# The second token half's input of the first norm, loaded with features on partitions

## The chip, the core and the metric

The kernel runs on one core of one Trainium2 chip. A core has five engines that run their own instruction streams: TensorE (PE in the profile, with its weight loads shown apart as PEld), VectorE (DVE), ScalarE (ACT), GpSimd (POOL) and SyncE (SP, which here issues most of the DMA transfers). On-chip memory has 128 partitions. The metric is the device time of one execution in microseconds; the kernel before takes 1170.82 us, the median of three runs.

## The reference, cut to what matters

One layer on 1024 tokens of 1024 features. The mixer has four gated-DeltaNet heads (projections q, k, v, z and the gates a and beta, a causal convolution on q, k, v, then a recurrence over chunks of 64 tokens) and a short convolution group; the change touches only the first line of the loop, the norm ahead of the mixer.

```
def rms_norm(x, w):
    x32 = x.astype(jnp.float32)
    y = x32 * lax.rsqrt(jnp.mean(x32 * x32, axis=-1, keepdims=True) + RMS_EPS)
    return (y * w.astype(jnp.float32)).astype(x.dtype)
...
    for l in range(DEPTH):
        mod = (c_act @ w_ada[l] + b_ada[l])[:, None, :]
        shift1, scale1, gate1, shift2, scale2, gate2 = jnp.split(mod, 6, axis=-1)
        h = rms_norm(x, norm1_w[l]) * (1.0 + scale1) + shift1
        x = x + gate1 * hybrid_mixer(h, w_in[l], conv_qkv_w[l], A_log[l], dt_bias[l],
                                     gdn_norm_w[l], conv_short_w[l], w_out[l])
        h = rms_norm(x, norm2_w[l]) * (1.0 + scale2) + shift2
        x = x + gate2 * swiglu(h, w_gate[l], w_up[l], w_down[l])
    return rms_norm(x, norm_f_w)
```

## The kernel before

**Tiles.** The tokens are handled in two halves of 512 (`HT`; half 0 and half 1), the features in eight blocks of 128 (`KB`). The mixer's input h is kept with features on partitions: for each block k and half hf a tile `H[k][hf]` of 128 features by 512 tokens, as a pair of a rounded high part and a low part that holds what the rounding lost. Every 32-bit product is three products of such parts (high by high, high by low, low by high), so a 128x512 result of the projection `w_in` (a tile `acc`) is 8 blocks times 3, that is 24 matmuls. In the row names h0 to h7 are such tiles of the input, u a weight pair, `cv` the result of a convolution, `raw` one of five staging tiles for weights on their way to a pair.

**The first norm.** For half 1, `h1_load` (line 799) loads four tiles x of 128 tokens by 1024 features and `xnorm` (263) scales each in place by its 1/rms: Square on ACT with a sum, add and power on POOL, a multiplication over 128x1024 on DVE. `h1_work` (809) then makes the eight blocks: four transposes on PE into one bank `tr`, and `h_make` (641) reads the bank twice (the high part on ACT; the full value `hf` on ACT or DVE), and DVE subtracts to get the low part. Half 0 does the same by other functions, ahead of it, and is not touched.

**What needs half 1.** `ab_phase(1)` (727) computes the gates of half 1 from all eight tiles H[k][1]. `gdn(hf)` (1203) follows for each half: preparations by head, then the recurrence, in which each chunk has four small products A (state by keys and queries), a DVE subtraction that writes the tile A anew, four products K (which update the state S on DVE) and four products O. So A, DVE, K, DVE and the next A are one chain. `fill` (924) carries the dense work: all products `acc` whose inputs are there, and when they are used up the products `o` of `w_out` for the first half: 8 blocks of 24 products, first for the output columns ch 1 of the token tiles x2_0 to x2_3, then for ch 0 of the same four.

```
        for ch, us in ((1, us1), (0, us0)):
            for i in range(4):
                ps = bank(dense, "o")
```

**After the recurrence.** When `gdn(1)` is done, `mod_rows` (1038) makes a row of the second norm's scale by four products `row`. It sets "row". `gate5(0)` and `gate5(1)` (1004) wait for that: each loads eight pieces of `w_ada` of 256 KB, which DVE adds up (tiles `aacc` and A), and splits the sum in two `Tt` or `raw` tiles. `norm0(t)` (964) waits for "row", both gates and both columns of tile t; it stores x2[t] to memory (`x_scr`), takes its rms, and scales it in place on DVE:

```
        dma(x2_scr[t], x2[t])
        junk = raw((P, D), BF16)
...
        DVE.scalar_tensor_tensor(x2[t], x2[t], st[:, 2:3], su[0][:, 0], ALU.mult, ALU.mult)
```

The scaling overwrites what the store reads, so it waits for the store.

**What sets the order.** Everything to this point is a set of threads that a planner (`Sim`, line 304) runs on the host while the program is built: each instruction costs what `cost` (373) says, each thread has a rank (`PR`, line 41: h1 1.8, chain 0, fill 9, a smaller number goes first), and the planner writes the instructions of every engine in the order in which its own clock reaches them. The chip then runs each engine's instructions strictly in that order, so a row that is not ready holds up all behind it. From the end of the planner's run (line 1508) the order is the code's own: the block `o` for the first tile of half 1 (24 products), four products row<-Tt on the split gate sums, 24 more of `o`, then 16 transposes `tr` of the scaled x2_0 to x2_3, and from there the second norm and the feed-forward part, which is most of the time left.

Of the kernel before, what the change touches and what calls it, by code (L numbers as in the profile page):

```python
# [9 lines left out]
F32 = mybir.dt.float32  # L10
F32R = mybir.dt.float32r
BF16 = mybir.dt.bfloat16
AF = mybir.ActivationFunctionType
# [38 lines left out]
def kernel(  # L52
    ctx: ExitStack,
    tc: tile.TileContext,
    x: bass.AP,
    c_cols: bass.AP,
    cols: bass.AP,
    w_ada: bass.AP,
# [46 lines left out]
    def nm(s):  # L105
        n_id[0] += 1
        return f"{s}_{n_id[0]}"
# [87 lines left out]
    def load_x(tt, pool, tag, bufs):  # L195
        t = pool.tile([P, D], F32, name=nm("x"), tag=tag, bufs=bufs)
        dma(t, xs[tt * P:(tt + 1) * P, :])
        return t
# [52 lines left out]
    nb1 = sp.tile([P, KB], F32, name="nb1", tag="nb1")  # L251
    mods = sp.tile([P, 2 * KB], F32, name="mods", tag="mods")

    def norm_rs(t, pool, tag, jt="junk"):
        junk = pool.tile([P, D], BF16, name=nm("jk"), tag=jt, bufs=1)
        st = pool.tile([P, 2], F32, name=nm("st"), tag=tag, bufs=4)
        sq = ACT.activation(junk, t, AF.Square, scale=1.0 / 32.0, accum_out=st[:, 0:1])
        p0 = POOL.tensor_scalar(st[:, 1:2], st[:, 0:1], EPS, None, ALU.add)
        rs = pool.tile([P, 1], F32, name=nm("rs"), tag=tag + "r", bufs=4)
        p1 = rsqrt_pow(rs, st[:, 1:2], 1)  # L260
        return rs, sq, p0, p1

    def xnorm(t, pool):
        rs = norm_rs(t, pool, "n1")[0]
        DVE.tensor_scalar(t, t, rs, None, ALU.mult)

    heads01 = [m0 + hd for hd in (0, 1) for m0 in (MT_K, MT_Q, MT_V)]
    late = []
# [296 lines left out]
    def bank(res, name):  # L565
        return res.tile(psp, [P, HT], F32, name)
# [23 lines left out]
    def tr(out_, in_):  # L590
        PE.transpose(out_, in_, ident)
# [202 lines left out]
        free(scr)  # L794
        sc_[hf] = dict(beta=beta, G=G, nG=nG, eG=eG, kd=kd)

    x1 = []

    def h1_load():
        sim.wait(lambda: "loads0" in done)  # L800
        for tt in range(4, 8):
            x1.append(load_x(tt, xp, "x", 8))
        for t in x1:
            xnorm(t, sp)
        done.add("x1")

    h1_left = list(range(KB))
# [1 line left out]
    def h1_work():  # L809
        sim.wait(lambda: "x1" in done)  # L810
        while h1_left:
            k = h1_left.pop(0)
            ps = bank(chb, "tr")
            for i in range(4):
                tr(ps[:, i * P:(i + 1) * P], x1[i][:, k * P:(k + 1) * P])
            h = h_slot(k, 1)
            h_make(k, h, ps)
            H[k][1] = h
            if all(H[j][1] is not None for j in range(KB)):
                done.add("h1")  # L820
# [1313 lines left out]
def _laid_out(a):  # L2134
    import numpy as np

    col = lambda v: v.reshape(-1, P).T
    w, wi = a["w_ada"][0], a["w_in"][0]
    d = {n: a[n] for n in ("x", "w_ada", "b_ada", "A_log", "dt_bias", "w_out", "w_gate", "w_up", "w_down", "norm_f_w")}
    d["c_cols"] = col(a["c"])  # L2140
    d["cols"] = np.concatenate([col(a[n]) for n in ("norm1_w", "b_ada", "norm2_w", "gdn_norm_w", "conv_qkv_w", "conv_short_w")], axis=1)
    d["w_mod"] = w[:, 0:2 * D].T.reshape(2, KB, P, D).transpose(1, 2, 0, 3)
    d["w_in0"] = wi[:, 0:1536].reshape(KB, P, 3, 512)[:, :, :, 0:256].reshape(KB, P, 768)
    main = np.concatenate([wi[:, 0:AB_COL], wi[:, SCB_COL:]], axis=1)
    d["w_in"] = main.reshape(KB, P, -1, P).transpose(2, 1, 0, 3).reshape(-1, P, D)
    d["w_ab"] = wi[:, AB_COL:SCB_COL].reshape(KB, P, 8).transpose(1, 0, 2).reshape(P, 64)
    d["consts"] = _constants()
    return d


_ARGS = ["x", "c_cols", "cols", "w_ada", "w_mod", "b_ada", "w_in0", "w_in", "w_ab", "A_log", "dt_bias", "w_out",
         "w_gate", "w_up", "w_down", "norm_f_w", "consts"]


# [34 lines left out]
```

## Time and profile before

| what | value |
|---|---|
| median of the runs (lowest, highest) | 1170.82 us (1170.20, 1170.95) |
| the profiled execution: its own time, its span | 1169.63 us, 1167.8 us |
| granted TensorE clock over the span | 0.999 |
| PE busy | 1157.2 us, 99% of the span |
| DVE, ACT, POOL busy | 920.7, 546.1, 59.6 us |
| instructions on PE, DVE, ACT, POOL | 5582, 1702, 1182, 100 |
| moved by DMA, mean rate | 207.06 MB, 177 GB/s |

Instructions are counted as the hardware's records have them; a 32-bit product with 128 columns has two records in some rows, so that "x8" of A or K is four products. A row of the timeline gives the start in the span, the length, the engine, the line of the code, the tile written and the tiles read, the shape and how many of a kind stand together, and in brackets the idle time ahead with what ended it. Lengths of neighbouring PE rows overlap, since a matmul's end is modelled; what a row costs is the distance to the next row's start. Lines 88, 89 and 450 are helpers that record instructions (450 those of the planner), so tiles tell more than lines.

### The profile page before, as it was taken

The numbers are of one execution on the slowest core, as the hardware profiler recorded it, in microseconds if no ns is written. First come the engines' busy times: TensorE is split into PE (matmuls) and PEld (weight loads), VectorE is DVE, ScalarE is ACT, GpSimd is POOL, SyncE is SP. The second block draws the span as 40 slices with busy tenths as digits, with TensorE's granted clock in tenths as the row PEclk, the third lists the DMA queues.
The fourth block names the chain that finished last, engine by engine and source line by source line (L and its number), as shares of the span: only waits on it lengthen the run. The fifth ranks groups of instructions, "written<-read, shape, count | busy, mean of one in ns | idle before, by whom it ended". The sixth has DMA issues, their size and how long they took to land.

```text
span 1167.8 us, 16456 instructions
## 1 busy us (share of the span) xinstructions
PE 1157.2 (99%) x5582; PEld 968.1 (83%) x5582; DVE 920.7 (79%) x1702; ACT 546.1 (47%) x1182; POOL 59.6 (5%) x100
## 2 busy tenths in 40 slices
PE   9999999999999999999999999999999999999997
PEld 7888888888888888888888888888888888888886
DVE  7898988898987898669776777776777687788676
ACT  6779733458634552325433333333333365443343
POOL 1110101001101010200000000000000000000002
PEclk9999999999999999999999999999999999999999
DMA  9633455534325555434264456446554589869413
GB/s 363 246 99 110 118 171 163 168 114 137 113 66 163 163 193 175 174 101 144 80 216 158 140 201 223 159 132 222 191 184 137 194 306 393 308 203 340 144 37 145
DMA packets 126453, 207.06 MB, mean 177 GB/s; under 512 B 20513, under 2 KB 45089, under 8 KB 126369
## 3 DMA queue, kind: packets, MB, share of 16 engines
q1 hardware_dynamic: 121520, 202.86, 51.5%
q10 hardware_dynamic: 4848, 3.15, 0.9%
q8 instruction: 44, 0.72, 0.3%
q14 instruction: 41, 0.33, 0.1%
HBM read 150.91 MB, written 55.05 MB: 176 GB/s over the span
## 4 chain that ended last, share of the span: by engine, by line
PE 93%; DVE 3%; ACT 2%; DMA 1%; issue 1%; SPq 0%; ACTq 0%; DVEq 0%
PE acc L88 35%; PE acc L450 24%; PE dn L88 17%; PE o L88 4%; PE o L450 4%; PE A L450 1%; PE K L450 1%; DMA wr<-in_w_in_dram 1%; DVE xo L89 1%; PE ab L450 1%; PE w L450 1%; PE u L450 1%; PE O L450 1%; PE tr L450 1%; PE kk L450 1%
## 5 line engine op out<-in xcount | busy, mean ns | idle before, releaser
L450 PE MATMUL acc<-h,u 128*128 128x512 f32 x1200 | 301.0, 398 | 0.0
L450 PEld LDWEIGHTS acc<-h,u 128*128 128x128 f32 x1200 | 219.0, 188 | 41.1
L88 PE MATMUL acc<-h,hl 128*128 128x512 f32 x600 | 140.1, 390 | 0.0
L88 PEld LDWEIGHTS acc<-h,hl 128*128 128x128 f32 x600 | 112.4, 188 | 23.2
L88 PE MATMUL acc<-h,u 128*128 128x512 f32 x456 | 106.1, 389 | 0.0
L88 PE MATMUL acc<-T,hl 128*128 128x512 f32 x432 | 101.4, 390 | 0.4 <-ACT cc L89 0.4
L88 PEld LDWEIGHTS acc<-h,u 128*128 128x128 f32 x456 | 85.6, 188 | 17.7
L88 PEld LDWEIGHTS acc<-T,hl 128*128 128x128 f32 x432 | 80.9, 188 | 17.5 <-ACT cc L89 0.9
L88 PE MATMUL dn<-h,h 128*128 128x512 f32 x396 | 90.7, 389 | 0.0
L89 DVE TENSOR_TENSOR xo<-xo,dn 128x512 f32<-128x512 f32 x84 | 57.0, 683 | 42.3 <-PE dn L88 34.8
L89 ACT COPY cc<-acc 128x512 f32<-128x512 f32 x66 | 38.4, 590 | 108.3 <-PE acc L88 108.3
L88 PEld LDWEIGHTS dn<-h,h 128*128 128x128 f32 x396 | 74.3, 188 | 15.4
L88 PE MATMUL acc<-T,u 128*128 128x512 f32 x360 | 84.0, 389 | 0.0
L88 PEld LDWEIGHTS acc<-T,u 128*128 128x128 f32 x360 | 67.6, 188 | 14.0
L450 ACT CAST u<-raw 128x512 fp32r<-128x512 f32 x69 | 42.7, 622 | 66.0 <-PE acc L450 64.3
L89 DVE TENSOR_TENSOR cc<-cc,acc 128x512 f32<-128x512 f32 x66 | 43.8, 682 | 29.8 <-PE acc L88 29.8
L89 DVE TENSOR_TENSOR hl<-R,hl 128x512 fp32r<-128x512 f32 x60 | 39.4, 687 | 33.5 <-ACT hl L89 33.4
L450 DVE TENSOR_TENSOR u<-raw,u 128x512 fp32r<-128x512 f32 x82 | 56.0, 685 | 11.9 <-ACT u L450 11.7
L450 DVE SCALAR_TENSOR_TENSOR cv<-pr,cols_a,cv 128x512 f32<-128x512 f32 x72 | 52.9, 745 | 0.1
L89 ACT CAST h<-rw 128x512 fp32r<-128x512 f32 x57 | 32.7, 618 | 40.5 <-PE dn L88 34.6
L89 ACT CAST hl<-R 128x512 fp32r<-128x512 f32 x60 | 35.7, 622 | 23.5 <-DVE R L89 10.7
L89 DVE TENSOR_TENSOR u<-R,u 128x512 fp32r<-128x512 f32 x46 | 30.1, 686 | 20.6 <-ACT u L89 20.5
(343 smaller groups left out, 1993.2 us busy)
## 6 DMA issues: line engine op xcount, KB each, us to landing
raw<-in_w_in_dram SPq DMA_DIRECT2D x82, 256.0 KB, 3.1
am_scr<-cc SPq DMA_DIRECT2D x77, 256.0 KB, 4.6
raw<-in_w_ada_dram SPq DMA_DIRECT2D x56, 256.0 KB, 3.4
rw<-am_scr SPq DMA_DIRECT2D x55, 256.0 KB, 5.2
rw<-bm_scr SPq DMA_DIRECT2D x53, 256.0 KB, 5.3
bm_scr<-raw SPq DMA_DIRECT2D x51, 256.0 KB, 5.4
R<-in_w_gate_dram SPq DMA_DIRECT2D x22, 512.0 KB, 4.3
R<-in_w_up_dram SPq DMA_DIRECT2D x22, 512.0 KB, 5.5
```

The costliest lines, as they stand in the source:

```text
L88: return call(*a, **k)
L89: ins = call(*a, **k)
L450: ins = call(*a, **k)
```

## The change

The input gets a second copy `x_t`, the second token half transposed on the host, 8 blocks of 128 features by 512 tokens. `h1_load` loads it as four tiles xt (two blocks each, 512 KB) and then loads the four row tiles x as before, since the squares still need them; they use the same eight slots. The four 1/rms columns go to one tile `rs1`; DVE multiplies the identity by them (a diagonal in a `raw` tile), one 32-bit product with a matrix of ones puts 1/rms of token c into column c of every partition (the bank `RS`), and a copy brings it to memory. A block is then made without PE: DVE multiplies xt by the scale column and by RS into `hf`, ACT adds the shift for the high part, and DVE takes (hf + shift) minus the high part for the low part. The 32 transposes, the four multiplications over 128x1024 and the second reading of the bank are gone.

```diff
--- before.py
+++ after.py
@@ -53,6 +53,7 @@
     ctx: ExitStack,
     tc: tile.TileContext,
     x: bass.AP,
+    x_t: bass.AP,
     c_cols: bass.AP,
     cols: bass.AP,
     w_ada: bass.AP,
@@ -251,18 +252,15 @@
     nb1 = sp.tile([P, KB], F32, name="nb1", tag="nb1")
     mods = sp.tile([P, 2 * KB], F32, name="mods", tag="mods")
 
-    def norm_rs(t, pool, tag, jt="junk"):
+    def norm_rs(t, pool, tag, jt="junk", rs=None):
         junk = pool.tile([P, D], BF16, name=nm("jk"), tag=jt, bufs=1)
         st = pool.tile([P, 2], F32, name=nm("st"), tag=tag, bufs=4)
         sq = ACT.activation(junk, t, AF.Square, scale=1.0 / 32.0, accum_out=st[:, 0:1])
         p0 = POOL.tensor_scalar(st[:, 1:2], st[:, 0:1], EPS, None, ALU.add)
-        rs = pool.tile([P, 1], F32, name=nm("rs"), tag=tag + "r", bufs=4)
+        if rs is None:
+            rs = pool.tile([P, 1], F32, name=nm("rs"), tag=tag + "r", bufs=4)
         p1 = rsqrt_pow(rs, st[:, 1:2], 1)
         return rs, sq, p0, p1
-
-    def xnorm(t, pool):
-        rs = norm_rs(t, pool, "n1")[0]
-        DVE.tensor_scalar(t, t, rs, None, ALU.mult)
 
     heads01 = [m0 + hd for hd in (0, 1) for m0 in (MT_K, MT_Q, MT_V)]
     late = []
@@ -794,14 +792,25 @@
         free(scr)
         sc_[hf] = dict(beta=beta, G=G, nG=nG, eG=eG, kd=kd)
 
-    x1 = []
+    x1t, rs1 = [], sp.tile([P, 4], F32, name="rs1", tag="rs1")
+    RS = sp.tile([P, HT], F32, name="RS", tag="RS")
 
     def h1_load():
         sim.wait(lambda: "loads0" in done)
-        for tt in range(4, 8):
-            x1.append(load_x(tt, xp, "x", 8))
-        for t in x1:
-            xnorm(t, sp)
+        for j in range(4):
+            t = xp.tile([P, 2, HT], F32, name=nm("xt"), tag="x", bufs=8)
+            dma(t, x_t[2 * j:2 * j + 2].rearrange("k p c -> p k c"))
+            x1t.append(t)
+        for i in range(4):
+            t = load_x(4 + i, xp, "x", 8)
+            norm_rs(t, sp, "n1", rs=rs1[:, i:i + 1])
+        dg = raw((P, 4, P))
+        DVE.tensor_tensor(dg, bc1(ident, 4), bc2(rs1, P), ALU.mult)
+        ps = bank(chb, "RS")
+        mm(ps, ones, flat(dg))
+        free(dg)
+        ecopy(RS, ps)
+        free(ps)
         done.add("x1")
 
     h1_left = list(range(KB))
@@ -810,11 +819,12 @@
         sim.wait(lambda: "x1" in done)
         while h1_left:
             k = h1_left.pop(0)
-            ps = bank(chb, "tr")
-            for i in range(4):
-                tr(ps[:, i * P:(i + 1) * P], x1[i][:, k * P:(k + 1) * P])
             h = h_slot(k, 1)
-            h_make(k, h, ps)
+            hf = hfs.tile(sp, [P, HT], F32, "hf")
+            DVE.scalar_tensor_tensor(hf, x1t[k // 2][:, k % 2], s1c[:, k:k + 1], RS, ALU.mult, ALU.mult)
+            ACT.activation(h[:, 0, :], hf, AF.Identity, bias=b1c[:, k:k + 1])
+            DVE.scalar_tensor_tensor(h[:, 1, :], hf, b1c[:, k:k + 1], h[:, 0, :].bitcast(F32), ALU.add, ALU.subtract)
+            free(hf)
             H[k][1] = h
             if all(H[j][1] is not None for j in range(KB)):
                 done.add("h1")
@@ -2137,6 +2147,7 @@
     col = lambda v: v.reshape(-1, P).T
     w, wi = a["w_ada"][0], a["w_in"][0]
     d = {n: a[n] for n in ("x", "w_ada", "b_ada", "A_log", "dt_bias", "w_out", "w_gate", "w_up", "w_down", "norm_f_w")}
+    d["x_t"] = a["x"][0, HT:].T.reshape(KB, P, HT)
     d["c_cols"] = col(a["c"])
     d["cols"] = np.concatenate([col(a[n]) for n in ("norm1_w", "b_ada", "norm2_w", "gdn_norm_w", "conv_qkv_w", "conv_short_w")], axis=1)
     d["w_mod"] = w[:, 0:2 * D].T.reshape(2, KB, P, D).transpose(1, 2, 0, 3)
@@ -2148,7 +2159,7 @@
     return d
 
 
-_ARGS = ["x", "c_cols", "cols", "w_ada", "w_mod", "b_ada", "w_in0", "w_in", "w_ab", "A_log", "dt_bias", "w_out",
+_ARGS = ["x", "x_t", "c_cols", "cols", "w_ada", "w_mod", "b_ada", "w_in0", "w_in", "w_ab", "A_log", "dt_bias", "w_out",
          "w_gate", "w_up", "w_down", "norm_f_w", "consts"]
```

As the planner runs again with these costs, the order of all engines changes. On PE, half 1's blocks stood among dense products in the order before (tr is the bank of a block, x the four row tiles; acc dense products of half 0):

```order
L450 MATMUL tr_956<-ident,x_405 128x128
L450 MATMUL tr_956<-ident,x_428 128x128
L450 MATMUL tr_956<-ident,x_436 128x128
L450 MATMUL tr_956<-ident,x_441 128x128
L450 MATMUL acc_892<-h_0_86_518,u_829 128x512 x3
L450 MATMUL acc_972<-h_0_37_238,u_858 128x512
L450 MATMUL tr_977<-ident,x_405 128x128
L450 MATMUL tr_977<-ident,x_428 128x128
L450 MATMUL tr_977<-ident,x_436 128x128
L450 MATMUL tr_977<-ident,x_441 128x128
L450 MATMUL acc_972<-h_0_37_238,u_858 128x512 x2
```

In the changed kernel no transposes stand there, and the one product RS stands earlier among products of the same kind:

```order
L448 MATMUL acc_710<-h_0_37_240,u_565 128x512 x3
L448 MATMUL acc_710<-h_0_44_274,u_565 128x512 x3
L448 MATMUL acc_710<-h_0_50_312,u_565 128x512 x3
L448 MATMUL acc_710<-h_0_56_350,u_565 128x512
L448 MATMUL RS_721<-raw_692,ones 128x512
L448 MATMUL acc_710<-h_0_56_350,u_565 128x512 x2
L448 MATMUL acc_710<-h_0_61_386,u_584 128x512 x3
L448 MATMUL acc_710<-h_0_70_432,u_584 128x512 x3
```

The dense products of half 0 thus follow one another without the groups of four transposes.

In the recurrence of half 1, PE has before, in one of its chunks, dense products between the products A and the products K that wait for what DVE makes of A:

```order
L450 MATMUL A_834_4479<-S_449_2398,WQ_546_2813 128x128
L450 MATMUL A_834_4479<-S_450_2400,WQ_547_2814 128x128
L450 MATMUL A_834_4479<-S_451_2403,WQ_548_2815 128x128
L450 MATMUL acc_824_4422<-h5_1_172_946,u_805_4326 128x512 x3
L450 MATMUL acc_824_4422<-h6_1_176_962,u_805_4326 128x512 x3
L450 MATMUL acc_824_4422<-h7_1_183_983,u_805_4326 128x512 x2
L450 MATMUL K_835_4489<-A_789_4244,kt_567_2947 128x128
L450 MATMUL K_835_4489<-A_789_4244,kt_618_3220 128x128
```

In the changed kernel one chunk (A_837 and K_842) has none there; the products `acc` are used up by then, and `o` is already the work with w_out:

```order
L448 MATMUL K_833_4498<-A_800_4334,kt_680_3558 128x128
L448 MATMUL o_824_4435<-wu_820_4400,h1_0_755_4053 128x512 x2
L448 MATMUL o_824_4435<-wu_829_4478,h2_0_762_4099 128x512 x3
L448 MATMUL A_837_4529<-S_444_2411,WQ_540_2828 128x128
L448 MATMUL A_837_4529<-S_445_2413,WQ_541_2829 128x128
L448 MATMUL A_837_4529<-S_446_2415,WQ_542_2830 128x128
L448 MATMUL A_837_4529<-S_448_2419,WQ_543_2831 128x128
L448 MATMUL K_842_4549<-A_800_4334,kt_565_2960 128x128
L448 MATMUL K_842_4549<-A_800_4334,kt_621_3259 128x128
L448 MATMUL K_842_4549<-A_800_4334,kt_650_3389 128x128
L448 MATMUL K_842_4549<-A_800_4334,kt_680_3558 128x128
```

So between A_837 and K_842 no other product stands on PE, where the chunk shown of before has eight. DVE has, ahead of the subtraction A<-u,A of the chunk shown of before (u<-O,qs is the output of the chunk before it, raw_826 and raw_831 weights of w_out that are scaled):

```order
L450 TENSOR_TENSOR u_626_3256<-O_830_4461,qs_814_4370 128x4x128
L450 SCALAR_TENSOR_TENSOR raw_826_4440<-raw_826_4440,cols_a_96,gate_246_1254 128x512
L450 TENSOR_TENSOR A_789_4244<-u_626_3256,A_834_4479 64x512
L450 SCALAR_TENSOR_TENSOR raw_831_4465<-raw_831_4465,cols_a_96,gate_246_1254 128x512
L450 TENSOR_TENSOR raw_832_4471<-raw_832_4471,gate_246_1254 128x512
```

and in the changed kernel, from the state updates that K_833 releases to the subtraction of A_837:

```order
L448 SCALAR_TENSOR_TENSOR S_444_2411<-S_444_2411,egl_536_2824,K_833_4498 128x128
L448 SCALAR_TENSOR_TENSOR S_445_2413<-S_445_2413,egl_537_2825,K_833_4498 128x128
L448 SCALAR_TENSOR_TENSOR S_446_2415<-S_446_2415,egl_538_2826,K_833_4498 128x128
L448 SCALAR_TENSOR_TENSOR S_448_2419<-S_448_2419,egl_539_2827,K_833_4498 128x128
L448 TENSOR_TENSOR raw_834_4504<-raw_834_4504,gate_304_1560 128x512
L448 SCALAR_TENSOR_TENSOR raw_816_4372<-raw_816_4372,cols_a_96,gate_304_1560 128x512
L448 TENSOR_TENSOR A_800_4334<-u_631_3304,A_837_4529 64x512
```

There, two scalings of weights stand between the state updates and the subtraction.

At the end of the recurrence, the four products `row` stand on PE in the first of the four blocks of ch 0 (o_900 belongs to x2_0; o_910, o_924 and o_935 to x2_1, x2_2 and x2_3):

```order
L450 MATMUL row_905_4889<-raw_903_4878,ones_79 128x512
L450 MATMUL o_900_4867<-h4_1_858_4640,h0_0_779_4188 128x512
L450 MATMUL o_900_4867<-h5_1_873_4703,h1_0_782_4201 128x512 x2
L450 MATMUL row_905_4889<-raw_904_4879,ones_79 128x512
L450 MATMUL o_900_4867<-h5_1_873_4703,h1_0_782_4201 128x512
L450 MATMUL o_900_4867<-h6_1_874_4720,h2_0_784_4210 128x512 x3
L450 MATMUL row_909_4906<-raw_907_4902,ones_79 128x512
L450 MATMUL o_900_4867<-h7_1_879_4738,h3_0_788_4234 128x512 x2
L450 MATMUL row_909_4906<-raw_908_4903,ones_79 128x512
L450 MATMUL o_900_4867<-h7_1_879_4738,h3_0_788_4234 128x512
L450 MATMUL o_910_4914<-h0_1_839_4514,h4_0_747_4040 128x512 x3
```

In the changed kernel they stand in the third of these blocks (o_896 belongs to x2_2, o_906 to x2_3):

```order
L448 MATMUL row_901_4908<-raw_899_4897,ones_79 128x512
L448 MATMUL o_896_4886<-h4_1_843_4555,h0_0_752_4042 128x512
L448 MATMUL o_896_4886<-h5_1_846_4575,h1_0_755_4053 128x512 x2
L448 MATMUL row_901_4908<-raw_900_4898,ones_79 128x512
L448 MATMUL o_896_4886<-h5_1_846_4575,h1_0_755_4053 128x512
L448 MATMUL o_896_4886<-h6_1_849_4588,h2_0_762_4099 128x512 x3
L448 MATMUL row_905_4925<-raw_903_4921,ones_79 128x512
L448 MATMUL o_896_4886<-h7_1_852_4620,h3_0_768_4128 128x512 x2
L448 MATMUL row_905_4925<-raw_904_4922,ones_79 128x512
L448 MATMUL o_896_4886<-h7_1_852_4620,h3_0_768_4128 128x512
L448 MATMUL o_906_4933<-h0_1_822_4420,h4_0_738_3960 128x512 x3
```

From the first `row` product to the first row<-Tt product, PE has 110 products of 512 columns before (the `row` products counted with them) and 62 in the changed kernel; from there to the transposes of x2 both have 28.

## The prediction

> **What bounds the kernel now.** I read the page first: how busy each engine is, the granted clock by slices, and the chain of work that ended last.
>
> ```profile
> span 1167.8 us, 16456 instructions
> PE 1157.2 (99%) x5582; PEld 968.1 (83%) x5582; DVE 920.7 (79%) x1702; ACT 546.1 (47%) x1182; POOL 59.6 (5%) x100
> ...
> PEclk9999999999999999999999999999999999999999
> ...
> PE 93%; DVE 3%; ACT 2%; DMA 1%; issue 1%; SPq 0%; ACTq 0%; DVEq 0%
> ```
>
> PE is busy 99% of the span at full clock in every slice, and the chain that ended last is PE in 93%. Then the waits of PE, which say whether anything else ever ends last:
>
> ```profile
> PE heat L88 <- POOL nhalf L89: 1.4, 1, 1.4
> PE acc L450 <- ACT h L450: 1.1, 1, 1.1
> PE acc L88 <- ACT cc L89: 0.4, 1, 0.4
> PE y L450 <- DVE pr L450: 0.4, 1, 0.4
> PE A L450 <- DVE S L450: 0.2, 1, 0.2
> PE ps L88 <- DVE raw L89: 0.2, 1, 0.2
> ```
>
> In all 3.7 us. So two things alone move the time: PE work taken away or added counts in full, and a new wait of PE counts in full. Work taken from DVE, ACT or DMA counts only where it ends such a wait. PE runs in a fixed order, so a row that is late holds up all behind it.
>
> **The PE work.** The transposes stand among dense products; the timeline of PE shows the last groups of half 1, and the only 32-bit products of 128x512 that the kernel has, in its opening.
>
> ```profile
> 85.36 0.60 PE L450 MATMUL tr<-ident,x 128*128 128x128 f32 x4
> 85.72 1.18 PE L450 MATMUL acc<-h,u 128*128 128x512 f32 x4
> 86.74 0.60 PE L450 MATMUL tr<-ident,x 128*128 128x128 f32 x4
> 87.09 2.56 PE L450 MATMUL acc<-h,u 128*128 128x512 f32 x10
> ...
> 3.70 2.61 PE L88 MATMUL ps<-raw,ones 128*128 128x512 f32 x4 [0.18 <-DVE raw L89]
> ```
>
> A group of four takes 85.72 - 85.36 = 0.36 and 87.09 - 86.74 = 0.35 us from start to start; eight groups are 8 x 0.355 = 2.84 us less. The product RS is of the kind of ps, which has two records each: 2.61 / 2 = 1.3 us in the opening. Later, a 32-bit product of 128 columns takes (412.59 - 411.78) / 4 = 0.20 us by the A row below, so 512 columns take 0.81. I take 0.9, near the lower end, since RS runs in the middle of dense work as A does. Net -1.9 us (-2.0 to -1.5).
>
> **DVE, ACT, POOL and SP in half 1's norm.** Gone are four DVE multiplications of 128x1024, seven readings of the bank on ACT and one on DVE; added are on DVE eight products for hf, the diagonal and the copy of RS; the low parts become two-operation forms. All lie beside PE's dense products; none is priced unless RS, or a first block of half 1, is late. RS waits for the rms of the last row tile. In before that came here:
>
> ```profile
> core 0: us, PE busy (x) PEld busy (x) DVE busy (x) ACT busy (x) POOL busy (x), PEclk, DMA share, GB/s
> 10.00:45.00 35.00, 33.85 (x178) 28.12 (x178) 30.04 (x50) 25.33 (x45) 2.83 (x5) 1.00 1.03 404
> 45.00:60.00 15.00, 15.00 (x69) 12.24 (x68) 13.21 (x31) 10.97 (x20) 3.23 (x6) 1.00 0.21 73
> ...
> 59.84 1.02 POOL L450 TENSOR_TENSOR rs<-st,nhalf 128x1 f32<-128x1 f32 x1
> ```
>
> The DMA engines are full until 45 us (404 GB/s) and nearly empty to 60. SP now issues 2 MB of xt ahead of the row tiles; 2 MB / 0.404 = 5.2 us more at full rate, which the empty stretch takes up. I estimate that the last rms still comes at about 60 to 61 us, the diagonal at 62.5, and that PE, by counting its products and their durations, reaches RS at 63.7. So nothing is added there, with a cover of about 1 us; if it is gone, see the third rival. The weights `w_in` behind these loads on SP come as much later; they are split several us ahead of use, so I price them at nothing.
>
> **The recurrence of half 1.** Without its stops the planner hands out dense products earlier, while its own times for the gates and the recurrence come later; its dense products are used up when the recurrence still needs cover. Before, eight of them stand between A and K:
>
> ```profile
> 411.78 1.05 PE L450 MATMUL A<-S,WQ 128*128 128x128 f32 x8
> 412.59 2.10 PE L450 MATMUL acc<-h,u 128*128 128x512 f32 x8
> 414.53 1.05 PE L450 MATMUL K<-A,kt 128*128 128x128 f32 x8
> 415.33 1.18 PE L450 MATMUL acc<-h,u 128*128 128x512 f32 x4
> ...
> 412.23 0.68 DVE L450 TENSOR_TENSOR u<-O,qs 128x512 f32<-128x512 f32 x1
> 412.83 0.74 DVE L450 SCALAR_TENSOR_TENSOR raw<-raw,cols_a,gate 128x512 f32<-128x512 f32 x1
> 413.49 0.67 DVE L450 TENSOR_TENSOR A<-u,A 64x512 f32<-64x512 f32 x1
> ...
> 415.62 1.12 DVE L450 SCALAR_TENSOR_TENSOR S<-S,egl,K 128x128 f32<-128x128 f32 x4 [0.19 <-PE K L450]
> 416.66 0.16 DVE L450 COPY ch<-halo_s 128x2 f32<-128x2 f32 x1
> ```
>
> From A<-u,A to K are 414.53 - 413.49 = 1.04 us; from the end of K (415.33) to S 0.29; S takes 1.04, a multiplication of two tiles 0.60, a two-operation form 0.66 (starts to starts). In the changed order nothing stands between A_837 and K_842, and DVE must do S, two scalings and then A<-u,A. Counted from the end of K_833: A<-u,A starts at 0.29 + 1.04 + 0.60 + 0.66 = 2.59, so K_842 at 3.63. PE is done with five `o` (1.15) and A_837 (0.81) at 1.96. It waits 1.67 us; taken 1.7. Were DVE free when A_837 is done (1.96 + 0.29), K_842 would come at 3.29, so 1.3 us is the floor; one more DVE pass of 0.7 ahead makes it 2.4. The other chunks keep at least six products there. Behind the waiting K on PE stands all the rest; DVE meanwhile goes on.
>
> **The end of the recurrence.** From the products `row` a chain runs that PE only meets again at row<-Tt and at the transposes of x2. Its rows on PE, SP and DVE:
>
> ```profile
> 454.31 0.40 PE L450 MATMUL row<-raw,ones 128*128 128x512 f32 x1
> ...
> 479.50 1.09 PE L88 MATMUL row<-Tt,ones 128*128 128x512 f32 x4
> ...
> 485.99 1.91 PE L88 MATMUL tr<-ident,x 128*128 128x128 f32 x16
> ...
> 454.74 0.33 SPq L450 DMA_DIRECT2D raw<-in_w_ada_dram  x1
> ...
> 466.07 9.08 SPq L450 DMA_DIRECT2D x_scr<-x  x4
> ...
> 469.51 0.67 DVE L450 TENSOR_TENSOR x<-x,o 128x512 f32<-128x512 f32 x1
> 470.11 0.68 DVE L450 TENSOR_TENSOR Tt<-A,Tt 128x512 fp32r<-128x512 f32 x1
> 470.71 0.68 DVE L450 TENSOR_TENSOR Tt<-aacc,Tt 128x512 fp32r<-128x512 f32 x1
> ...
> 475.98 4.96 DVE L450 SCALAR_TENSOR_TENSOR x<-x,st,u 128x1024 f32<-128x1024 f32 x4 [1.17 <-ACT raw L450]
> ```
>
> SP's loads of w_ada start when the first `row` product frees a staging tile (454.31, 454.74); the stores of x2 follow at 466.07. What the loads feed ends with Tt at 471.39, 17.1 us after `row`; the four scalings of x2 end at 480.94, 26.6 us after. PE arrived at 479.50 and 485.99: covers of 8.1 and 5.1 us. PE's 110 products from `row` to row<-Tt took 25.19, 0.229 each. In the changed order there are 62, so 14.2 us, and 28 more, so 20.6 us to the transposes. The length of the chain itself hardly changes: it starts at the same `row`, and one x<-x,o of 0.6 us fewer stands ahead of Tt. So row<-Tt waits about 16.5 + 0.2 - 14.2 = 2.5 us, and the transposes for the rest: 26.6 + 0.1 - 0.3 (the three before the one that reads x2_3) - 20.6 = 5.8 in all, 5.7 taken for the fewer DVE operations. Its upper end is 6.1. Its lower end depends on what released the first scaling, at 475.98. The profile names ACT's Square, but this scaling overwrites what the store issued at 466.07 reads, and that landed after 9.8 us:
>
> ```profile
> x_scr<-x SPq DMA_DIRECT2D x1, 512.0 KB, 9.8
> ```
>
> 466.07 + 9.8 = 475.9. I hold to the store, which keeps its distance from `row`. Were the scalings free as soon as Tt is done, they would end at 16.5 + 5.0 = 21.5, and only the wait at row<-Tt would remain, 2.5 us.
>
> The Trainium skill, "DMA: Bandwidth & Descriptors", section "Anatomy of one DMA", has about 2 us fixed and the bytes at up to 436 GB/s; for a 512 KB store I estimate 3.2 us from it. By that the store would land at 469.3, the scalings would not wait for it, and the sum would be +2.3 in place of +5.5. The trace does not agree here: the store took 9.8 us, behind other transfers.
>
> **The sum.** -1.9 + 1.7 + 5.7 = +5.5 us. Against the profiled execution's own 1169.63 us this is 1175.1; that execution lies 1.2 us (0.1%) below the median, so against the median of 1170.82 it is 1176.3.
>
> **The rivals.**
>
> First, the tail waits only at row<-Tt. For it: ACT's Square is what the profile names as releaser, and it ended at the same time as the store. Against it: a store that is read from under the scaling. Then -1.9 + 1.7 + 2.5 = +2.3, 1173.1.
>
> Second, and not slower: the chain behind `row` shortens with its cover, since the transfers that set it come sooner. In the changed order three of the four x2 tiles are complete when the stores are issued, where the stores of before were spread over 9.08 us, and the first piece may be loaded earlier. The tail then costs nothing and -1.9 + 1.7 = -0.2 is left, 1170.6. It decides from the point where the four scalings end less than 20.6 us after `row`, and Tt less than 14.2, instead of 26.6 and 17.1. Against it: 16 pieces of w_ada, four loads and four stores are 8.4 MB, and at 0.404 that alone is 20.8 us before the last store has landed.
>
> Third, the opening: x rows are late behind 2 MB of xt, RS is not ready at 63.7, and PE waits for it and then for the first blocks of half 1. For it: the DMA engines are full to 45 us, and a row tile needs a slot that half 0's transposes free. Each us later than my estimate plus 1 counts in full; 2 to 4 us make 1178 to 1180.
>
> A fourth bears on the size of the stop alone: PE may come back from a long stop at a lower clock. No row here shows it, as the longest wait is 1.4 us and the clock is full in every slice; half speed for as long as the longest stop of 3.3 us would add 1.7 us, 1178. The Trainium skill, "TensorE: Matmul & The Clock Gate", section "Part 1", says that an idle window of about 3.4 us halves the clock. No run here shows it yet.
>
> **How the numbers follow.** The sum has 0.56, the first rival 0.14, the second 0.10, the third 0.12, the fourth 0.08. A measurement of this kernel tells 0.2%, 2.3 us, from no change: 1168.5 to 1173.2. The first rival lies at that bound and is split; the second lies inside, and I give 0.04 of it to a case where the wait of K goes too and PE's saving is larger than counted. So faster 0.04; same 0.06 + 0.10 = 0.16 (the 0.10 from the first rival and the low end of the sum); slower 0.80. The range reaches down to the first rival with the sum's lower ends (-1.9 + 1.3 + 2.5, less a little) and up over the upper ends (-1.5 + 2.4 + 6.1 = +7.0, 1177.8) into the third and fourth: 1171.5 to 1179.5. The second rival and half of the third lie outside.
>
> **What would show it.** In the profile of the changed kernel: PE busy about 1155; a wait of K for DVE's A near 1.7 us; a wait of row<-Tt for Tt near 2.5, and of tr for x2 near 3.2; SP's first w_ada load right behind `row`, and the first x<-x,st,u about 21.7 us behind it; RS without idle time ahead. The prediction is wrong if the waits of PE stay below 5 us in all, if RS or the first acc on half 1 waits, or if a wait stands where I counted none, above all at the products y or in the recurrence of half 0.

## The result and the profile after

The changed kernel takes 1175.43 us (median of six runs, 1174.47 to 1176.39), the kernel before 1170.26 in the same measurement: a ratio of 1.0043, 95% interval 1.0030 to 1.0056, slower by 5.2 us. The forecast was 1176.3, range 1171.5 to 1179.5. The profiled execution took 1175.39 us, its span 1173.6, 5.8 us more than the span before.

The page of the changed kernel, and below it the whole list of PE's waits (us in total, times, longest):

```profile
span 1173.6 us, 16403 instructions
...
PE 1157.8 (99%) x5552; PEld 966.8 (82%) x5552; DVE 923.0 (79%) x1710; ACT 539.9 (46%) x1174; POOL 61.3 (5%) x100
```

```profile
PE row L89 <- ACT Tt L448: 2.4, 1, 2.4
PE tr L89 <- DVE x L448: 1.8, 2, 0.9
PE K L448 <- DVE A L448: 1.5, 1, 1.5
PE heat L89 <- POOL nhalf L90: 1.4, 1, 1.4
PE acc L448 <- ACT h L448: 1.2, 1, 1.2
PE row L89 <- DVE Tt L448: 0.2, 1, 0.2
```

The three waits that the forecast named are the three that are new: row<-Tt 2.4 + 0.2, the transposes tr, and K. The timeline of PE shows the places, RS first:

```profile
61.78 2.20 PE L448 MATMUL acc<-h,u 128*128 128x512 f32 x9
63.82 1.02 PE L448 MATMUL RS<-raw,ones 128*128 128x512 f32 x2
64.28 1.95 PE L448 MATMUL acc<-h,u 128*128 128x512 f32 x6
...
416.65 1.39 PE L448 MATMUL o<-wu,h 128*128 128x512 f32 x5
417.92 1.26 PE L448 MATMUL A<-S,WQ 128*128 128x128 f32 x8
420.68 1.16 PE L448 MATMUL K<-A,kt 128*128 128x128 f32 x8 [1.50 <-DVE A L448]
421.60 1.15 PE L448 MATMUL o<-wu,h 128*128 128x512 f32 x3
422.59 0.40 PE L448 MATMUL o<-L,h 128*128 128x512 f32 x1
...
464.05 0.40 PE L448 MATMUL row<-raw,ones 128*128 128x512 f32 x1
...
478.11 0.40 PE L89 MATMUL o<-wu,kt 128*128 128x512 f32 x1
480.91 0.50 PE L89 MATMUL row<-Tt,ones 128*128 128x512 f32 x1 [2.40 <-ACT Tt L448]
481.63 0.97 PE L89 MATMUL row<-Tt,ones 128*128 128x512 f32 x3 [0.23 <-DVE Tt L448]
...
488.00 0.72 PE L89 MATMUL tr<-ident,x 128*128 128x128 f32 x2
489.62 0.33 PE L89 MATMUL tr<-ident,x 128*128 128x128 f32 x1 [0.90 <-DVE x L448]
490.84 3.03 PE L89 MATMUL tr<-ident,x 128*128 128x128 f32 x13 [0.89 <-DVE x L448]
493.53 0.62 PE L89 MATMUL o<-L,WQ 128*128 128x512 f32 x1
```

RS runs without idle time ahead of it and takes 64.28 - 63.82 = 0.46 us. From the first `row` to the end of the transposes are 493.53 - 464.05 = 29.48 us; before they were 33.34 (454.31 to 487.65, from the row of the 16 transposes and the 1.66 us to the next), with 48 products more. 48 x 0.229 = 11.0, so without stops it would have been 22.35: the tail lost 7.1 us. The rows of DVE that end these waits:

```profile
416.92 0.69 DVE L448 TENSOR_TENSOR h<-raw,h 128x512 fp32r<-128x512 f32 x1
417.53 1.11 DVE L448 SCALAR_TENSOR_TENSOR S<-S,egl,K 128x128 f32<-128x128 f32 x4
...
480.89 0.69 DVE L448 TENSOR_TENSOR Tt<-aacc,Tt 128x512 fp32r<-128x512 f32 x1
485.84 4.94 DVE L448 SCALAR_TENSOR_TENSOR x<-x,st,u 128x1024 f32<-128x1024 f32 x4 [4.26 <-POOL st L448]
```

Tt is done 17.5 us behind the first `row`, the scalings start 21.8 and end 26.7 behind it (17.1, 21.7 and 26.6 before): the chain kept its length while its cover (the PE work between the chain's start and the row that needs its end) fell. And behind the stops at the transposes the clock went down, in a view by stretches (us, busy time and count of PE, PEld, DVE, ACT, POOL, then the granted clock, the DMA share and GB/s):

```profile
488.00:490.00 2.00, 0.93 (x4) 0.28 (x2) 2.00 (x3) 0.00 (x0) 0.00 (x0) 1.00 0.17 68
490.00:492.00 2.00, 1.16 (x6) 1.16 (x7) 2.00 (x4) 0.00 (x0) 0.00 (x0) 0.61 0.00 0
492.00:494.00 2.00, 2.00 (x11) 1.96 (x10) 1.17 (x2) 0.35 (x1) 0.00 (x0) 0.54 0.35 131
494.00:496.00 2.00, 2.00 (x10) 1.65 (x9) 0.20 (x1) 2.00 (x5) 0.79 (x2) 1.00 0.35 131
```

Of the 16 transposes the last 13 took 493.53 - 490.84 = 2.69 us, where 16 took 1.66 before. In finer stretches the granted clock is 0.50 from 490.4 to 493.8, and 1.00 ahead of it and behind it. Behind the stops at row<-Tt and at K it stays at 1.00.

### The profile page after: what moved, and what is told of

It reads as the page before. It is cut to its first block, busy times and chain, and to the rows that moved or that the text cites. A ratio compares the mean times of both kernels' runs of the same rounds, so it can differ in the third digit from the quotient of the medians.

```text
span 1173.6 us, 16403 instructions
## 1 busy us (share of the span) xinstructions
PE 1157.8 (99%) x5552; PEld 966.8 (82%) x5552; DVE 923.0 (79%) x1710; ACT 539.9 (46%) x1174; POOL 61.3 (5%) x100
## 4 chain that ended last, share of the span: by engine, by line
PE 93%; DVE 3%; DMA 2%; ACT 1%; issue 0%; SPq 0%; ACTq 0%; DVEq 0%
PE acc L89 35%; PE acc L448 26%; PE dn L89 17%; PE o L448 3%; PE o L89 3%; PE K L448 1%; PE A L448 1%; DMA Tt<-in_w_ada_dram 1%; DMA x_scr<-x 1%; PE ab L448 1%; DVE xo L90 1%; PE u L448 1%; PE w L448 1%; PE qk L448 1%; PE kk L448 1%; PE O L448 1%
## 5 line engine op out<-in xcount | busy, mean ns | idle before, releaser
L448 PE MATMUL acc<-h,u 128*128 128x512 f32 x1200 | 295.2, 396 | 0.0
L89 PE MATMUL acc<-h,u 128*128 128x512 f32 x456 | 106.1, 389 | 0.0
```

What stands on the lines that cost most here:

```text
L89: return call(*a, **k)
L448: ins = call(*a, **k)
```

## The experiments

All are measured against the kernel before in the same measurement (its medians there: 1170.9 for e1 to e4, 1170.35 for e5 to e8, 1170.5 for e9 and e10).

| run | edit | median, us | ratio to before (95%) |
|---|---|---|---|
| changed kernel | | 1175.43 | 1.0043 (1.0030 to 1.0056) |
| e1 | changed, rank of half 1's blocks 1.1 | 1168.75 | 0.9981 (0.9971 to 0.9991) |
| e2 | before, rank 1.1 | 1176.33 | 1.0042 (1.0027 to 1.0057) |
| e3 | changed, order of the tail | 1174.43 | 1.0028 (1.0018 to 1.0037) |
| e4 | changed, stores of the tail not of x2 | 1172.46 | 1.0015 (1.0005 to 1.0026) |
| e5 | changed, order of the tail, second form | 1169.07 | 0.9990 (0.9981 to 1.0000) |
| e6 | changed, stops filled | 1173.85 | 1.0033 (1.0020 to 1.0046) |
| e7 | changed, rank 1.25 | 1166.29 | 0.9967 (0.9955 to 0.9978) |
| e8 | before, two DVE passes a block | 1170.43 | 1.0004 (0.9995 to 1.0014) |
| e9 | changed, one DVE pass a block | 1169.35 | 0.9988 (0.9979 to 0.9998) |
| e10 | before, rank 1.25 | 1171.72 | 1.0013 (1.0004 to 1.0022) |

**e1 and e2: the rank of half 1's blocks.** One number of the planner's table, in the changed kernel (e1) and in the kernel before (e2):

```diff
-... out=4, h1=1.8, split=3, ...
+... out=4, h1=1.1, split=3, ...
```

> The changed kernel with one number of the planner's ranks altered: the blocks of half 1 (h1) go from 1.8 to 1.1, ahead of the gates and of the reading of finished products. In its order the gates of half 1 stand 20.7 us of PE work earlier than in the changed kernel, eight products stand between every A and K, and PE has 28.2 us of work from `row` to row<-Tt and 34.6 us to the transposes of x2 (changed kernel 14.2 and 20.6, kernel before 25.2 and 31.6). Theory of lost cover: the waits of K, row<-Tt and tr and the low clock behind them are gone, and PE's saving of 2.4 us (32 transposes at 0.0885 less RS at 0.46) shows: 1170.3 - 2.4 = 1167.9, faster than before. Rival, that the norm without transposes costs time of itself (more DVE work, the transfers in the opening): waits stand elsewhere, 1172 to 1175. Rival of the opening: RS stands 2.1 us earlier on PE than in the changed kernel, and its diagonal, done at 62.98 there, may be late: up to 1.3 us of idle time ahead of RS, 1169.

> The kernel before with the same number altered (h1 1.8 to 1.1), as a control: transposes and all as before, gates of half 1 18.5 us of PE work earlier. The covers behind A and behind `row` were enough before and are a little larger here (27.3 and 33.7 us). Theory of lost cover: nothing to gain, within 0.2% of before. Rival, that the rank is worth time of itself whatever the norm: faster by 2 us or more, and then e1 says nothing about the transposes.

e1 is faster than the kernel before, 1168.75 against the forecast 1167.9, and none of the three waits is left. e2, the control, did not stay where it was: it is slower by 5.4 us. Its timeline has a stop where the gates of half 1 are asked for, and its stretches a low clock behind it:

```profile
84.52 0.30 PE L450 MATMUL gT<-ident,ghl 128*128 128x128 f32 x1 [3.23 <-DVE raw L450]
85.78 2.08 PE L450 MATMUL acc<-h,u 128*128 128x512 f32 x4 [0.97 <-ACT pr L450]
```

```profile
84.50:86.00 1.50, 0.52 (x2) 0.34 (x3) 1.50 (x3) 0.92 (x3) 0.00 (x0) 0.83 0.00 0
86.00:88.00 2.00, 2.00 (x5) 1.60 (x6) 1.77 (x10) 1.96 (x4) 0.00 (x0) 0.50 0.01 4
```

So the rank is not worth time of itself; with the old norm it costs, since I had counted only the covers behind A and `row` and not that of the gates. With the new norm it gives the cover back and PE's saving shows.

**e3 and e5: the tail's order.** Both leave the planner's part alone and move the code's own order behind it. e3:

```diff
     w_out_tile(4, 1)
     keep_x2(4, (1,))
-    g5_rows()
     w_out_tile(4, 0)
+    g5_rows()
     norm_tile(4)
-    first_half(range(4))
     w_out_tile(5, 1)
     keep_x2(5, (1,))
+    first_half(range(4))
     first_half(range(4, 8))
```

> The changed kernel with the code's own order behind the planner altered alone: the second block of the first tile of half 1 goes ahead of the row<-Tt products, and the first block of the second tile ahead of the transposes of x2. PE then has 19.7 us of work from `row` to row<-Tt and 26.1 us to the transposes; the chain needs 16.9 and 26.8 (as measured in the changed kernel). Theory: the wait at row<-Tt (2.6) is gone, the one at the transposes shrinks to under 0.6, and without long stops the clock stays full: of the 7.1 us that the tail lost, 6.5 come back, 1168.9. The wait of K (1.5) stays. Rival, that the stop only moves to what follows (the transposed blocks come later and the feed-forward part waits for them): 1170 to 1173.

The waits at row<-Tt and at the first transposes are gone, but the gain was only 1 to 2 us (1.0 by the medians, 1.8 by the ratios): with 32 transposes in a row PE stopped ahead of the last four of them and again behind them, as the rival had it.

```profile
495.58 0.66 PE L89 MATMUL tr<-ident,x 128*128 128x128 f32 x4 [1.95 <-DVE x L90]
497.46 3.04 PE L89 MATMUL o<-h,WQ 128*128 128x512 f32 x12 [1.22 <-DVE h L90]
```

Its ten executions spread over 3.9 us, and the longer ones have the lower granted clock (mean over the span):

```
time, us        1171.85 1172.75 1173.50 1173.81 1174.29 1174.58 1175.17 1175.31 1175.53 1175.78
granted clock     0.999   0.998   0.998   0.998   0.997   0.995   0.995   0.995   0.996   0.995
```

A mean that is lower by 0.004 over some 1170 us is worth 4.7 us at full clock (an estimate), about as much as the times differ. Only the execution of 1171.85 us has a profile, and in it the clock is 1.00 behind these stops; that the same stops lower it in the others is not shown by a row. The spread alone would say nothing: the kernel before reached from 1169.52 to 1173.74 in the same measurement, but at 0.998 to 0.999 throughout. e5 puts the second tile's second block between the two groups of transposes:

```diff
     first_half(range(4))
+    w_out_tile(5, 0)
+    norm_tile(5)
     first_half(range(4, 8))
     early_load(0)
     early_load(1)
     sums_x(0)
-    w_out_tile(5, 0)
-    norm_tile(5)
```

(on top of e3's edit)

> The changed kernel with the code's own order behind the planner altered as in e3, but with the second block of the second tile between the two groups of 16 transposes, where e3 had 32 transposes in a row and stopped again behind them (1.9 + 1.2 us). Theory of lost cover: the stops of the tail are gone but for about 0.5 us ahead of the first transposes, no low clock follows, 1175.4 - 7.1 + 0.6 = 1168.9, with all executions within 1 us. Rival, that the tail's later steps have no room left whatever the order: a stop of 1 to 3 us stands somewhere in the second norm or at the start of the feed-forward part, 1171 to 1174.

1169.07, against 1168.9: 6.4 of the tail's 7.1 us are back, all executions within 2.5 us. Its waits are those of the opening and K (and 0.2 us later on), and the transposes run at full speed:

```profile
490.73 1.91 PE L89 MATMUL tr<-ident,x 128*128 128x128 f32 x16
498.05 1.91 PE L89 MATMUL tr<-ident,x 128*128 128x128 f32 x16
```

That shows the tail to be a matter of cover alone: the same products, 24 or 48 of them moved ahead of the point where PE waited.

**e4: what holds the scalings.**

```diff
-        dma(x2_scr[t], x2[t])
+        dma(x2_scr[t], xs[t * P:(t + 1) * P, :])
```

> The changed kernel, but the four stores that keep x2 before it is scaled (x2_0 to x2_3) copy the input x instead of x2, so that the scaling need not wait for them; the same bytes go through the same queue. This leaves the mixer's output out of the residual of the first four tiles. Theory (the store releases the first scaling): it starts at about 483 instead of 485.8, when its rms is done, the four end at about 488, the transposes wait under 0.3 us, the clock stays full there, and 2.5 + 1.4 us come back: 1171.5. The wait at row<-Tt and that of K stay. Rival (ACT's Square or POOL releases it, as the profile's names have it): the scalings start at the same time, no change, 1175.4.

DVE's rows, with the first `row` at 464.34:

```profile
482.54 1.29 DVE L448 SCALAR_TENSOR_TENSOR x<-x,st,u 128x1024 f32<-128x1024 f32 x1 [1.33 <-POOL st L448]
484.89 2.48 DVE L448 SCALAR_TENSOR_TENSOR x<-x,st,u 128x1024 f32<-128x1024 f32 x2 [1.06 <-POOL st L448]
487.83 1.29 DVE L448 SCALAR_TENSOR_TENSOR x<-x,st,u 128x1024 f32<-128x1024 f32 x1 [0.46 <-POOL st L448]
```

The first scaling starts 18.2 us behind `row` instead of 21.8, so it was the store that held it. The records that the profile names as the releaser (ACT's Square before, done at 475.9; POOL's st in the changed kernel, done at 485.8) are by their times those of the last tile; the first tile's own rms was done at 472.3 and at 482.9, 3 us or more ahead of its scaling. In e4 the rest is then held by POOL, one by one, and ends 24.8 behind `row`, not at the 23.7 that I expected, so that the transposes still wait 1.1 us; 3 of the 4 us came back, 0.7 of them at row<-Tt, which came 16.2 us behind `row` instead of 16.9.

**e6: filling the stops.**

```diff
+    def fill_stop(n):
+        ps = allb.get("fs")
+        for i in range(n):
+            pmm(ps, Y[1][KORD[0]][0][:, 0:P], us0[KORD[0]][0], i == 0, i == n - 1)
     w_out_tile(4, 1)
     keep_x2(4, (1,))
+    fill_stop(11)
     g5_rows()
     w_out_tile(4, 0)
     norm_tile(4)
+    fill_stop(11)
     first_half(range(4))
```

> The changed kernel with products of no use put into the two stops of the tail: 11 of 512 columns (2.5 us) ahead of row<-Tt and 11 ahead of the first transposes; nothing else is altered, and the waits on DVE end when they did. Theory that the stops themselves lower the clock: it stays full through the tail, the 13 transposes behind the stop take 1.2 us instead of 2.7, the row<-Tt products 0.9 instead of 1.5, the time is 1175.4 - 1.5 to 2.0 = 1173.5 to 1174, and the executions lie closer together. Rival, that the slow stretch has another cause (the freshly written operands, the weight loads): it stays, and the time is the same or up to 0.3 us more, 1175.4 to 1175.7.

1173.85, in the range of the theory, though its executions lie hardly closer together (1.6 us, 1.9 in the changed kernel). The 16 transposes run at full speed and so do the row<-Tt products (0.93 us for the four instead of 1.53, of which 0.23 was a wait); the clock is 1.00 through:

```profile
486.87 2.73 PE L89 MATMUL fs<-h,WQ 128*128 128x512 f32 x11
489.43 1.91 PE L89 MATMUL tr<-ident,x 128*128 128x128 f32 x16
491.10 0.47 PE L89 MATMUL o<-L,WQ 128*128 128x512 f32 x1
```

With 22 products more that compute nothing, the tail from the first `row` (463.50) to the end of the transposes takes 27.6 us instead of 29.5. The time is 1.6 us lower; as the two come from different measurements and the intervals of their ratios overlap (1.0020 to 1.0046 and 1.0030 to 1.0056), it is the rows that show the gain. So the slow rows came from the idle time: of the tail's 7.1 us some 5.4 are waits and some 1.7 are rows that ran slower behind them, 1.3 the transposes at half the clock and 0.4 the row<-Tt products. The latter ran slower at a granted clock of 1.00; why is open.

**e8 and e9: what moved the order.** e8 takes the kernel before and gives its blocks the second DVE pass; e9 takes the changed kernel and gives them one.

```diff
-            h_make(k, h, ps)
+            hf = hfs.tile(sp, [P, HT], F32, "hf")
+            ACT.activation(h[:, 0, :], ps, AF.Identity, bias=b1c[:, k:k + 1], scale=s1c[:, k:k + 1])
+            DVE.tensor_scalar(hf, ps, s1c[:, k:k + 1], b1c[:, k:k + 1], ALU.mult, ALU.add)
+            free(ps)
+            DVE.tensor_tensor(h[:, 1, :], hf, h[:, 0, :].bitcast(F32), ALU.subtract)
+            free(hf)
```

> The kernel before, transposes and all, with one thing of the change's cost: the full value hf of half 1's blocks is always made by DVE, so that DVE has two passes for each block, as in the changed kernel (before, ACT made hf in seven of eight). In its order the gates of half 1 stand 5.5 us of PE work later than in the kernel before, and the covers fall from 25.2 to 19.0 us (row<-Tt) and from 31.6 to 25.4 us (transposes); every A keeps eight products. Theory that the second DVE pass at a low rank is what delays half 1 and eats the cover: row<-Tt needs 17.1 and does not wait, the transposes need 26.8 and wait about 1.2 us, so 1170.9 + 1.2 = 1172.1, up to 1173 with a low clock. Rival, my reading in the prediction (the missing transposes let the dense work run ahead): with the transposes there nothing moves, 1170.9.

```diff
-            DVE.scalar_tensor_tensor(hf, x1t[k // 2][:, k % 2], s1c[:, k:k + 1], RS, ALU.mult, ALU.mult)
-            ACT.activation(h[:, 0, :], hf, AF.Identity, bias=b1c[:, k:k + 1])
-            DVE.scalar_tensor_tensor(h[:, 1, :], hf, b1c[:, k:k + 1], h[:, 0, :].bitcast(F32), ALU.add, ALU.subtract)
+            xk = x1t[k // 2][:, k % 2]
+            ACT.activation(hf, xk, AF.Identity, bias=b1c[:, k:k + 1], scale=s1c[:, k:k + 1])
+            ACT.activation(h[:, 0, :], xk, AF.Identity, bias=b1c[:, k:k + 1], scale=s1c[:, k:k + 1])
+            DVE.tensor_tensor(h[:, 1, :], hf, h[:, 0, :].bitcast(F32), ALU.subtract)
```

> The changed kernel (no transposes, xt loaded, RS made) with one DVE pass for a block in place of two: ACT makes the full value and the high part from xt, DVE subtracts, as before the change. This leaves 1/rms out of half 1's h (RS is made and not used). The rank of the blocks stays at 1.8. In its order the gates of half 1 stand 17.9 us of PE work earlier than in the changed kernel, and the covers are 27.9 and 34.4 us, with eight products behind every A. Theory that the second DVE pass at a low rank delays half 1 and eats the cover: no stop in the recurrence or the tail, PE's saving of 2.4 us shows and perhaps more as in e7, 1166 to 1168.5. Rival, my reading in the prediction (without the transposes as stops the dense work runs ahead of the chains): the transposes are gone here too, so the covers would be short and the time 1173 or more.

e8's transposes of x2 wait 1.2 us for the scalings, as forecast, and nothing else in the tail waits:

```profile
487.56 0.38 PE L88 MATMUL tr<-ident,x 128*128 128x128 f32 x2
488.27 0.33 PE L88 MATMUL tr<-ident,x 128*128 128x128 f32 x1 [0.33 <-DVE x L450]
489.52 1.64 PE L88 MATMUL tr<-ident,x 128*128 128x128 f32 x13 [0.91 <-DVE x L450]
```

The time does not tell 1.2 us: 1.0004, 0.9995 to 1.0014, which holds 1.001. e9 has no stop in the recurrence of half 1 or in the tail, with the transposes gone as in the changed kernel. It is faster than before by 1.2 us, not by 2 to 4: small waits of 0.2 to 1.0 us stand at y, gT and P instead, and with those of the opening they add up to 6.3 us in its profiled execution (the longest of the ten), where the kernel before had 3.7. Its blocks no longer read RS, but that gave them no more than 1.3 us: the first starts at 64.98, in the changed kernel at 66.30. Together the two runs show the larger part of the cause. With one pass the cover stays though the transposes are gone (27.9 us behind `row`), so the second DVE pass is needed for the loss. With two passes and the transposes there, it falls from 25.2 to 19.0, which is 6.2 of the 11.0 us that the change takes from it (to 14.2), and every A keeps its eight products. The rest of the loss, and the stop of K, came only with both; which part of the change adds it is not shown. What goes with the loss both times is the second DVE pass, behind work of a better rank, in a stretch where DVE is nearly full (from 60 to 100 us it is busy for 38.5 us in the changed kernel, 35.5 before). In the changed kernel the last low part of half 1 is made at 98.93, before at 89.34 (rows of DVE, the changed kernel's first):

```profile
98.93 0.74 DVE L448 SCALAR_TENSOR_TENSOR h<-hf,b1c,h 128x512 fp32r<-128x512 f32 x1
```

```profile
89.34 0.69 DVE L450 TENSOR_TENSOR h<-hf,h 128x512 fp32r<-128x512 f32 x1 [0.38 <-ACT hf L450]
```

**e7 and e10: a rank between.** As e1 and e2, with 1.25, which leaves the gates (1.2) ahead of the blocks.

> The changed kernel with the rank of half 1's blocks at 1.25, behind the gates (1.2) and ahead of the reading of finished products (1.5), where e1 had 1.1. The covers are those of the kernel before (25.2 us from `row` to row<-Tt, 31.6 to the transposes, eight products behind every A). Theory: PE's saving of 2.4 us again, 1168.5 (1167.9 by the kernel before alone, and e1 measured 1168.75), and no wait above 1 us but the opening's. Rival: the place of the gates matters as it did in e2 (a stop of 3 us ahead of them), 1172.

> The kernel before with the rank of half 1's blocks at 1.25, the control for e7. Covers 28.2 and 34.6 us, eight products behind every A, gates of half 1 19.7 us of PE work earlier than in the kernel before and 9.3 earlier than in e7. If the rank alone were what e7 gained, this would be about 1166.3 + 2.4 = 1168.7. If the gates then come before their inputs, as in e2 (a stop of 3.2 + 1.0 us ahead of gT and a low clock behind it), 1174 to 1177, and only the changed norm can use the rank.

e7 is the fastest version here, 1166.29, 3.9 us below the kernel before by the ratio (0.9967), better than my 1168.5. All its waits of PE:

```profile
PE heat L89 <- POOL nhalf L90: 1.4, 1, 1.4
PE acc L448 <- ACT h L448: 0.5, 1, 0.5
PE ada L448 <- DVE qs L448: 0.2, 1, 0.2
```

PE's saving of 2.4 us and waits of 2.1 instead of 3.7 make 4.0. The kernel before does not gain by the same number: 1171.72, 0.1% slower. Neither of my two values for e10 came (1168.7, or 1174 and more); it has no stop as e2 had, and its waits add up to 3.6 us, as before. What makes it 1.2 us slower is open: in its profile PE is busy for 1159.6 us instead of 1157.2 with the same products, so it is rows that take longer and not waits. Between e10 and e7, which differ by the change alone, lie 5.4 us, 3 more than PE's saving (in the profiles 4.3 of PE's busy time, 1159.6 against 1155.3, and 1.5 of waits); that too is not settled by a row.

## Why the prediction was right

By its own steps, with the profiled executions (+5.8 us in the span):

| step | forecast, us | measured, us | from |
|---|---|---|---|
| 32 transposes less, RS more | -1.9 | -2.4 | RS 0.46 instead of 0.9 |
| K behind A with nothing between | +1.7 | +2.4 | K late by 1.95 from start to start (a wait of 1.5 in the profile's count), slower rows behind it 0.4 |
| the tail | +5.7 | +7.1 | waits of about 5.4, slower rows about 1.7, of which 1.3 at half the clock |
| the rest | 0 | -1.3 | waits elsewhere of 2.6 us instead of 3.7 make 1.1 of it |

The waits stand where the forecast counted them, and each is held by the chain that it named. That the time came out within 0.3 us of the span's +5.8 is in part luck: the three priced steps make +7.1 where I had +5.5, and the -1.3 elsewhere, which I had not forecast, took most of that back.

- RS was mis-sized. I scaled from products of 128 columns (0.20 each); one of 512 takes 0.46, so the short ones don't scale by their columns. The bound of 0.81 was no lower bound.
- K: from 417.92 to 422.59 are 4.67 us for work that takes 0.81 + 0.81 + 0.69 without a stop. DVE did S, two scalings and A<-u,A in a row, as counted; K came 4.03 us behind the end of K_833 (416.65) instead of 3.63, as DVE still had a low part to make (416.92) when S was released, the one more pass that the upper end of the term had counted; K then followed A<-u,A by 0.74 instead of 1.04. The granted clock is 1.00 there.
- The tail's waits came out within 0.3 us of the sum (at the transposes 2.5 us from start to start, 1.8 in the profile's count, 3.2 forecast). The choice that carried it, the store as what releases the first scaling, was right against the profile's own name (e4). The store took 9.4 us to land in the changed kernel:

```profile
x_scr<-x SPq DMA_DIRECT2D x1, 512.0 KB, 9.4
```

  The sum of +2.3 did not come: the store stands among the loads issued just ahead of it, and from 476 to 486 us the DMA engines are full (a share of 0.96 to 1.01); no run takes these loads away. The 3.2 us that I had estimated from the Trainium skill, "DMA: Bandwidth & Descriptors", section "Anatomy of one DMA", come from a fit that the section gives for transfers issued by GpSimd, where these stores are issued by SP. With the store as releaser the first rival falls; the second, a shorter chain, too: it kept its 26.7 us.
- The third rival, a late RS, did not come: no idle time ahead of RS at 63.82, forecast for 63.7. The fourth, a lower clock behind a long stop, came on top of the sum; I had given it 0.08 as a case of its own, and it belonged into the term. Here the clock fell to 0.50 at 490.4, 2.4 us after the dense products had ended at 488.0, and in these PE made three transposes; no single stop was longer than 2.6 us. In e2 it fell at 85.4, behind a stop of 3.2 us and one product gT; both times it stayed low for 3.4 us. The Trainium skill, "TensorE: Matmul & The Clock Gate", section "Part 1", has the clock halve after an idle window of about 3.4 us, and that window runs freely and does not start with the kernel. The trace agrees with the half speed; it does not agree with 3.4 us of full idleness as the condition, since PE still ran dense products 2.4 us ahead of the fall. That a freely running window is why e3's executions differ is not shown.
- PE's busy time was forecast at 1155 and is 1157.8: the rows that run slower behind the stops count as busy. In e1 and e7, which have no such stops, it is 1154.6 and 1155.3.
- One reason was wrong though its number was right: that the order changes "without its stops", the transposes. e8 and e9 show the second DVE pass of each block, at a rank behind the reading of finished products, as what comes late; the dense work runs ahead of chains that start later. I had put down that DVE work as hidden, and its cost on DVE was; by its effect on the order behind it, it takes more than half of the lost cover by itself (e8), and without it no cover is lost (e9).

## What to carry to other kernels

Where a planner or a table sets the order, a change that takes work from the bound engine can lose more than it saves by moving the order: count, in the new order, the bound engine's work between each chain's start and its end, and set it against the chain's length in the old trace; that gave the waits of the tail to within 0.3 us before a run, though not the slower rows behind them. When such a cover falls short, look for the rank of the work that became late before giving up the change: here one number made of +5.2 us a gain of 3.9. And what holds a chain may be the store that reads a tile about to be overwritten, though the profile names another engine.

## What the runs showed of the hardware

A stop can cost more than its length. Behind the stops at the transposes of the changed kernel (2.8 us with three transposes in them) and behind e2's stops of 3.2 and 1.0 us, the granted clock was 0.50 for 3.4 us; behind the single stop of 2.4 us at row<-Tt, and in the profiled execution of e3 behind stops of 1.9 and 1.2 us, it stayed at 1.00. Filling the stops of the tail with useless products of the same length made the tail 1.9 us shorter (e6). The clock differs between executions of one kernel (e3: 1171.85 us at a mean clock of 0.999, 1175.78 at 0.995). A 32-bit product of 512 columns took 0.46 us where four of 128 columns take 0.81.
